# One set of key transposes a step later, the last head's products among the output projection's, and a norm broadcast three products later, in a two-layer hybrid attention trunk

## The chip, the cores and the metric

The kernel runs on one core of a Trainium2 chip. The metric is the device time of one execution in microseconds (us). Within a core five engines run side by side, each taking its own instructions strictly in their written order: PE multiplies matrices into PSUM banks, ACT applies functions and copies, DVE does element-wise arithmetic, POOL does the same for small side work, and SP starts the DMA transfers.

## What is computed

Two layers on 256 tokens of width 1024, in float32:

```python
h = h + 0.5 * swiglu(rms_norm(h, ffn1_norm[l]), ffn1_w_gate[l], ffn1_w_up[l], ffn1_w_down[l])
h = h + hybrid_mixer(rms_norm(h, mix_norm[l]), w_in[l], ..., w_out[l], cos, sin)
h = h + 0.5 * swiglu(rms_norm(h, ffn2_norm[l]), ffn2_w_gate[l], ffn2_w_up[l], ffn2_w_down[l])
```

A feed-forward block (FFN) has hidden width 2816. The mixer projects once with `w_in` and then has three head groups: A, four query heads that attend to the 64 keys per query which an indexer with eight small heads picks; B, four heads with plain causal attention at this length; C, eight heads with a forget bias and an output gate. Their 16 outputs are joined and multiplied by `w_out`.

## The kernel before

**Precision.** Each float32 matrix is split into a rounded part and a remainder (`wh`, `wl` for weights, `xhl` or `h`, `l` for activations), and three products stand for one. Weights come in by DMA as `raw`; ACT writes `wh` (L116), DVE subtracts to get `wl` (L120). `W.pump()` issues one such pair, up to seven units ahead of use; `W.take()` hands a unit to PE.

**Order.** It is written by hand: the order of the Python calls is the order on each engine. PSUM has eight banks, handed out in turn from two groups of four, "gu" and "acc"; a bank is written again only when its last readers are done.

**FFN.** For each of 22 tiles of the hidden width, `proj()` makes eight 512-wide products with `wh` and eight 256-wide ones with `wl` into one "gu" bank, once for the gate and once for the up matrix. The norm's scale is applied late: `norm.sums` (squares summed by PE), then a power on POOL (`y_n`, L304), then `norm.broadcast`, two small PE products that spread the scale over all partitions, copied by ACT into `rb` (L349). In every FFN but the first, `sums` is issued inside the first up group and `broadcast` inside the second gate group, each as a callback after one of the `wl` products. `gated` multiplies by `rb`.

**Mixer.** The projection runs in eight chunks of four units; after each unit a step counter goes up and `run_side` issues whatever is due at that step, in order of due time and then of registration, then one `W.pump()`. So the attention of group B and the indexer of A lie between the projection's products. The due steps that matter here: the last indexer sums and `cumsum` (which writes a bank that DVE reads at L763 and L764) at 16; `topk` rounds, two maxima and two replacements on DVE (L739, L741), at 17, 19, 21 and so on; `bq_turn` and `bk_turn` at `B_TURN` = 18; the first scores of B at 20. `bq_turn` multiplies the stacked queries by an identity (`identr`). `bk_turn` is `keys_T` with two "acc" banks: per bank four PE transposes (L626), an ACT cast (L628) and a DVE subtraction (L629), giving `bkT` high and low.

**End of the mixer.** A loop over the 12 heads of A and C interleaves their scores, `flip` (transposes of the probabilities, L920, copied as `pT`, L922), `values` (probabilities times values, then a reciprocal and scaling on DVE) and `outT` (two heads' outputs transposed, L953, and split by ACT L960 and DVE L961) with the output projection's first five inputs. `tail` does the last three inputs for the four pairs of output tiles (`mp` 0 to 3): products, then `residual` on DVE (L352), `nxt.high` on ACT (L317), `nxt.low` on DVE (L320), and the squares for the next norm. The last input needs the last `outT`, so for the first two pairs the products of the other two inputs are issued ahead of it:

```python
        if late:
            part(0, ks[:-1])
            late()
            part(1, ks[:-1])
        for mp in range(4):
            ms = (2 * mp, 2 * mp + 1)
            part(mp, ks[-1:] if late and mp < 2 else ks)
```

The next FFN's first `proj` follows directly; it takes inputs 0 to 5 first and 6 and 7 afterwards.

Of the kernel before, what the change touches and what calls it, by code (L numbers as in the profile page):

```python
# [36 lines left out]
OUT_TAIL = 3  # L37
WARM = 7
B_TURN, B_STEP, A_ROOT, A_TURN = 18, 20, 22, 26
# [12 lines left out]
OUT_ORDER = [2, 3, 0, 1, 4, 5, 6, 7]  # L52
# [88 lines left out]
def kernel(ctx: ExitStack, tc: tile.TileContext, x, ffn1_norm, ffn1_w_gate, ffn1_w_up, ffn1_w_down,  # L141
# [17 lines left out]
    def bank(tag):  # L159
        return psum.tile([P, 512], F32, name="ps_" + tag, tag=tag)  # L160

    def tmp(n):
        return tp.tile([P, 512], F32, name="tmp", tag="tmp")[:, :n]
# [128 lines left out]
    def mm(o, l, r, start, stop):  # L292
        T.matmul(o, l, r, start=start, stop=stop, skip_group_check=True)  # L293

    def mm3(o, lhs, rhs, start, stop):
        mm(o, lhs[0], rhs[0], start, False)
        mm(o, lhs[0], rhs[1], False, False)
        mm(o, lhs[1], rhs[0], False, stop)
# [52 lines left out]
    def residual(acc, m, n, factor):  # L351
        V.scalar_tensor_tensor(hres[:, m:m + n], acc[m // 2].rearrange("p (a b) -> p a b", a=2)[:, m % 2:m % 2 + n],  # L352
                               factor, hres[:, m:m + n], op0=ALU.mult, op1=ALU.add)


    def ffn(norm, nxt, aside=None, g0=None):
# [50 lines left out]
        def proj(between=None, after=0, tag="gu", groups=(range(KT),)):  # L407


            w = W.take()  # L410
            ps = bank(tag).rearrange("p (a b) -> p a b", a=2)
            for ks in groups:
                for k in ks:
                    mm(ps, w[0][:, k], norm.x[:, k], k == 0, False)
                for k in ks:
                    mm(ps[:, 0], w[1][:, k], norm.h[:, k], False, k == KT - 1)
                    if between and k == after:
                        between()
            return ps
# [35 lines left out]
        if first:  # L455
            u0 = proj()
            g1 = proj(norm.sums, 6)
            W.pump()
            W.low()
            for mp in range(1, 4):  # L460
                V.tensor_copy(hres[:, 2 * mp:2 * mp + 2], xT[mp])
            u1 = proj(norm.broadcast, 6)
            W.pump(2)
            early[2] = proj(tag="acc")
        else:
            g0 = proj(groups=(range(6), range(6, KT)))
            W.pump()
            u0 = proj(norm.sums, 5)
            W.pump(2)
            g1 = proj(norm.broadcast, 4)  # L470
            W.pump()
            u1 = proj()
        early[1] = g1
# [5 lines left out]
        acc = [bank("acc") for _ in range(4)]  # L479
        for f in range(1, NF):  # L480
# [6 lines left out]
            if f == 8 and aside:  # L487
                aside()
        ks = list(range(NF - DOWN_LAG, NF))
        return tail(acc, hid, ks, 0.25, nxt) if nxt else finish(ks)  # L490

    def tail(acc, rhs, ks, factor, make_norm, late=None):

        nxt = make_norm()
        ws = dict(zip(ks, [W.take() for _ in ks]))

        def part(mp, some):
            for k in some:
                for m in (2 * mp, 2 * mp + 1):
                    mm3(acc[mp][:, (m % 2) * S:(m % 2 + 1) * S], [v[:, 0, m * P:(m + 1) * P] for v in ws[k]],  # L500
                        rhs[k], False, k == ks[-1])

        if late:
            part(0, ks[:-1])
            late()
            part(1, ks[:-1])
        for mp in range(4):
            ms = (2 * mp, 2 * mp + 1)
            part(mp, ks[-1:] if late and mp < 2 else ks)
            for m in ms:  # L510
                if mp == 3:
                    residual(acc, m, 1, factor)
                elif m == ms[0]:
                    residual(acc, m, 2, factor)
                nxt.high(m)
            if late and mp == 0:
                continue
            for m in ((0, 1) if late and mp == 1 else ()) + ms:
                nxt.low(m)
            for p in (([0] if late and mp == 1 else []) + ([mp - 1] if mp > 1 or (mp == 1 and not late) else [])  # L520
                      + ([3] if mp == 3 else [])):
                nxt.squares(p)
        W.pump()
        return nxt
# [23 lines left out]
    def mixer(l, norm, nxt):  # L548
# [3 lines left out]
        def at_step(n, fn):  # L552
            side.append((n, next(count), fn))
# [7 lines left out]
        def heads(ap, n):  # L561
            return ap.rearrange("p (h d) -> p h d", h=n)

        def rope(x, ta, tb, E=G):

            n = x.shape[1]
            bc = lambda a: a[:, None, :].to_broadcast([P, n, a.shape[1]])
            b = tp.tile([P, S], F32, name="swapped", tag="swapped", bufs=2)
            b = heads(b[:, :n * HD], n)
            G.tensor_tensor(b[:, :, 0:32], x[:, :, 32:64], bc(tb[:, 0:32]), op=ALU.mult)  # L570
            G.tensor_tensor(b[:, :, 32:64], x[:, :, 0:32], bc(tb[:, 32:64]), op=ALU.mult)
            E.tensor_tensor(x, x, bc(ta), op=ALU.mult)
            E.tensor_tensor(x, x, b, op=ALU.add)
# [6 lines left out]
        def squares(ps, t, n):  # L580
            sq = tmp(64 * n)
            A.activation(sq, ps, AF.Square, scale=norm.r[:, t:t + 1])
            return heads(sq, n)

        def square_sums(ss, sq):
            V.tensor_reduce(ss, sq, axis=AX.X, op=ALU.add)

        def head_rs(ss, n, tag):
            return rsqrt(ss, ss, 1.0 / HD, n, tag)
# [6 lines left out]
        def evac(dst, ps, t, scale=None):  # L596
            A.activation(dst, ps, AF.Copy, scale=norm.r[:, t:t + 1])
# [206 lines left out]
        def post_b(ps):  # L804
            ss = sm.tile([P, 2, 4], F32, name="ssbk", tag="ss")
            rot = [hp.tile([P, S], F32, name="bkr", tag="hl") for _ in range(2)]
            sq = []
            for t in range(2):
                evac(rot[t], ps[t][:, :256], t)
                evac(va[t][:, 1:5, 0:64], heads(ps[t][:, 256:512], 4), t)  # L810
                sq.append(squares(ps[t][:, :256], t, 4))
                rope(heads(rot[t], 4), tab[:, 3, 0, t], tab[:, 3, 1, t])

            def bk_norm():
                for t in range(2):
                    square_sums(ss[:, t], sq[t])
                rs = head_rs(ss.rearrange("p t h -> p (t h)"), 8, "bk")
                for t in range(2):
                    twice = tmp(512).rearrange("p (h s d) -> p h s d", h=4, s=2)
                    G.tensor_tensor(twice, heads(rot[t], 4)[:, :, None, :].to_broadcast([P, 4, 2, HD]),  # L820
                                    rs[:, 4 * t:4 * t + 4, None, None].to_broadcast([P, 4, 2, HD]), op=ALU.mult)
                    bk.append(twice.rearrange("p h s d -> p h (s d)"))

            def bk_turn():
                st["bkT"] = at.tile([P, 2, 4, S], F32R, name="bkT", tag="kT")
                keys_T(st["bkT"], bk)

            bk = []
            at_step(13, bk_norm)
            at_step(B_TURN, bk_turn)  # L830

            def qk_b(kind, h):
                return st["bqT"][:, h], [st["bkT"][:, c, h] for c in range(2)]

            run_heads([("B", h) for h in range(4)], qk_b, "acc", lambda i, fn: at_step(B_STEP + i, fn), 2)
# [137 lines left out]
        oT = {}  # L973
        posts = dict(iq=post_iq, ib=post_ib, a=post_a, b=post_b, ck=post_ck, cq=post_cq, cv=post_cv, cg=post_cg)
        for name, cols in CHUNKS:
            n = sum(c[1] for c in cols)
# [20 lines left out]
        acc = [bank("acc") for _ in range(4)]  # L997
# [32 lines left out]
        scores, exps, flip, values, outT = run_heads(hs, qk_ac, "gu")  # L1030
        n = len(hs)
        next(halves)
        for i in range(n + 1):
            if i < n:
                scores(i)
            if i > 0:
                flip(i - 1)
            if i < n:
                exps(i)
            if i in (3, 5, 7, 9):  # L1040
                c_T((i - 3) // 2)
            if i not in (3, 5, 9, n):
                next(halves)
            if i > 0:
                values(i - 1)
                if i > 2 and i % 2:
                    outT((i - 3) // 2)
        for _ in halves:
            raise AssertionError
        return tail(acc, oT, OUT_ORDER[8 - OUT_TAIL:], 1.0, nxt, lambda: outT(n // 2 - 1))  # L1050


    def before_mixer(l):
# [12 lines left out]
    norm = Norm(0, 0)  # L1066
# [35 lines left out]
    for mp in range(4):  # L1102
        ks = range(2 * mp, 2 * mp + 2)
# [30 lines left out]
    for l in range(DEPTH):  # L1134
        norm = ffn(norm, lambda: Norm(1, l), lambda: before_mixer(l), g0 if l == 0 else None)
        norm = mixer(l, norm, lambda: Norm(2, l))
        norm = ffn(norm, (lambda: Norm(0, l + 1)) if l + 1 < DEPTH else None)
# [35 lines left out]
```

## Time and profile before

| what | us |
|---|---|
| median of 3 runs (lowest, highest) | 1061.42 (1061.30, 1061.51) |
| the profiled execution | 1061.49 |
| its span from first to last instruction | 1059.7 |
| PE busy | 1049.7 |
| DVE busy | 829.2 |
| ACT busy | 594.1 |

The profile records one execution. A timeline row has the start in us from the span's beginning, the time, the engine, the line, the operation, output and inputs, and the count of instructions merged into the row; in brackets stands how long the engine stood idle before it and what ended that. A row of the waits has the waiter, who released it, the sum, the count and the longest. A windows row has, for each engine, busy time and instruction count, then the granted TensorE clock, DMA share and GB/s. Mean granted clock over the run is 0.998.

### The profile page before, as it was taken

To read this page: it belongs to the slowest core of one execution; us is meant where nothing else is said; L and a number is where in the kernel's file an instruction comes from. 1 tells how busy PE (TensorE), PEld (TensorE's weight loads), DVE (VectorE), ACT (ScalarE), POOL (GpSimd) and SP (SyncE) were. 2 spreads that over 40 slices of the span, in tenths; PEclk is the share of its full clock that TensorE was granted. 3 is DMA by queue.
4 is the path that set the end of the run, shared out by engine and by line. 5 is a ranking of instruction groups with operands and counts; after the bars stand their busy time and mean duration, and the time that the engine had idled before them with its cause. 6 is when DMAs were issued, how large, how long until landed. Compare 5 with 4: busy or idle time off the path is not lost.

```text
span 1059.7 us, 16913 instructions
## 1 busy us (share of the span) xinstructions
PE 1049.7 (99%) x6611; PEld 950.5 (90%) x6611; DVE 829.2 (78%) x1568; ACT 594.1 (56%) x1018; POOL 164.1 (15%) x184
## 2 busy tenths in 40 slices
PE   9999999999999999999999999999999999999998
PEld 8999999998899899999989999999978998888887
DVE  6998777779876887777789777778798779877774
ACT  6665554667654665555456555547766555655551
POOL 2004000267700100000010300003765000000000
PEclk9999999999999999999999999999999999999999
DMA  9576464465441365464546555454455214564531
GB/s 328 202 242 202 161 228 154 133 221 169 134 148 41 120 238 187 171 220 143 195 159 221 183 200 188 171 185 167 159 170 185 84 41 163 198 234 163 198 119 40
DMA packets 130913, 181.81 MB, mean 172 GB/s; under 512 B 7009, under 2 KB 104721, under 8 KB 130833
## 3 DMA queue, kind: packets, MB, share of 16 engines
q1 hardware_dynamic: 130512, 180.65, 50.4%
q8 instruction: 52, 0.85, 0.3%
q14 instruction: 29, 0.23, 0.1%
q10 hardware_dynamic: 320, 0.08, 0.0%
HBM read 179.67 MB, written 1.05 MB: 171 GB/s over the span
## 4 chain that ended last, share of the span: by engine, by line
PE 62%; DVE 2%; ACT 1%; issue 1%; POOL 0%; POOLq 0%; ACTq 0%; DVEq 0%
PE ps_gu L293 41%; PE ps_acc L293 20%; DVE score L721 0%; PE ps_gu L920 0%; PE ps_gu L1020 0%; DVE wl L120 0%; DVE xhl L320 0%; DVE hres L352 0%; ACT xhl L317 0%; PE ps_acc L383 0%; ACT tmp L329 0%; POOLq L1169 0%; POOL y_n L304 0%; PE ps_gu L953 0%; PE ps_acc L920 0%
## 5 line engine op out<-in xcount | busy, mean ns | idle before, releaser
L120 DVE TENSOR_TENSOR wl<-raw,wh 128x1024 fp32r<-128x1024 f32 (+2 forms) x343 | 416.0, 1219 | 21.8 <-ACT wh L116 21.8
L293 PE MATMUL ps_gu<-xhl,wh 128*128 128x512 f32 (+1 forms) x1408 | 351.9, 392 | 0.2 <-DVE tmp L425 0.2
L116 ACT CAST wh<-raw 128x1024 fp32r<-128x1024 f32 (+2 forms) x343 | 344.6, 1033 | 7.6 <-PE ps_gu L293 3.3
L293 PEld LDWEIGHTS ps_gu<-xhl,wh 128*128 128x128 f32 x1408 | 253.8, 189 | 46.0 <-DVE tmp L425 0.4
L293 PEld LDWEIGHTS ps_gu<-xhl,wl 128*128 128x128 f32 x1400 | 192.1, 191 | 13.7
L293 PE MATMUL ps_gu<-xhl,wl 128*128 128x256 f32 x1400 | 198.0, 283 | 0.0
L293 PE MATMUL ps_gu<-wh,xhl 128*128 128x512 f32 (+2 forms) x512 | 159.5, 382 | 0.0
L425 DVE TENSOR_TENSOR tmp<-ps_gu,tmp 128x256 f32<-128x256 f32 x175 | 74.0, 423 | 106.6 <-ACT tmp L424 106.5
L293 PE MATMUL ps_acc<-hl,wh 128*128 128x256 f32 x528 | 150.0, 284 | 0.0
L293 PE MATMUL ps_acc<-hh,wl 128*128 128x256 f32 x528 | 149.7, 283 | 0.0
L293 PE MATMUL ps_acc<-hh,wh 128*128 128x256 f32 x528 | 149.6, 283 | 0.0
L424 ACT COPY tmp<-ps_gu 128x256 f32<-128x256 f32 x175 | 64.6, 369 | 132.8 <-PE ps_gu L293 126.9
L293 PEld LDWEIGHTS ps_gu<-wh,xhl 128*128 128x128 f32 x512 | 95.7, 190 | 14.7
L293 PEld LDWEIGHTS ps_acc<-hl,wh 128*128 128x128 f32 x528 | 101.5, 192 | 0.3
L293 PEld LDWEIGHTS ps_acc<-hh,wh 128*128 128x128 f32 x528 | 101.5, 192 | 0.0
L293 PEld LDWEIGHTS ps_acc<-hh,wl 128*128 128x128 f32 x528 | 101.5, 192 | 0.0
L293 PE MATMUL ps_gu<-wl,xhl 128*128 128x512 f32 (+2 forms) x256 | 96.5, 377 | 0.0
L331 POOL TENSOR_TENSOR ssacc<-ssacc,tmp 128x512 f32<-128x512 f32 x10 | 13.0, 1296 | 510.8 <-ACT tmp L329 332.2
L432 ACT ACTIVATE tmp<-tmp 128x256 f32<-128x256 f32 x88 | 36.8, 418 | 85.2 <-DVE tmp L430 85.2
L441 ACT CAST hh<-tmp 128x256 fp32r<-128x256 f32 x80 | 32.6, 408 | 86.6 <-DVE tmp L437 86.6
L293 PEld LDWEIGHTS ps_gu<-wl,xhl 128*128 128x128 f32 x256 | 48.7, 190 | 6.7
L430 DVE TENSOR_TENSOR tmp<-tmp,rb 128x256 f32<-128x256 f32 x88 | 37.8, 429 | 3.0
(247 smaller groups left out, 1231.8 us busy)
## 6 DMA issues: line engine op xcount, KB each, us to landing
raw<-in_ffn_w_down_dram SPq DMA_DIRECT2D x44, 1024.0 KB, 7.2
raw<-in_ffn_w_gate_dram SPq DMA_DIRECT2D x43, 1024.0 KB, 7.4
raw<-in_ffn_w_up_dram SPq DMA_DIRECT2D x43, 1024.0 KB, 5.0
raw<-in_w_in_dram SPq DMA_DIRECT2D x24, 1024.0 KB, 5.0
raw<-in_w_out_dram SPq DMA_DIRECT2D x8, 1024.0 KB, 4.8
raw<-in_w_in_dram SPq DMA_DIRECT2D x4, 768.0 KB, 4.8
raw<-in_w_in_dram SPq DMA_DIRECT2D x4, 656.0 KB, 4.4
xin<-in_x_dram SPq DMA_DIRECT2D x4, 256.0 KB, 5.0
```

The costliest lines, as they stand in the source:

```text
L116: self.nc.scalar.copy(hv, src)
L120: (engine or self.nc.vector).tensor_tensor(lv, self.srcs[self.n_low], hv.bitcast(F32), op=ALU.subtract)
L293: T.matmul(o, l, r, start=start, stop=stop, skip_group_check=True)
L331: G.tensor_tensor(self.acc, self.acc, sq, op=ALU.add)
L424: A.copy(o, ps[:, 1])
L425: V.tensor_tensor(o, ps[:, 0], o, op=ALU.add)
L430: V.tensor_tensor(t_, t_, norm.rb, op=ALU.mult)
L432: A.activation(th, t_, AF.Tanh, scale=0.5)
L441: (V.tensor_copy if late else A.copy)(hh, t_)
```

## The change

Three edits, each acting in several places. `bk_turn` moves from step 18 to step 19, where it is registered behind that step's `topk`; this happens in both mixers. In the loop over heads the last `values` is no longer issued right behind the last `flip`; `tail` now issues the early products of three pairs, with the last `values` behind those of pair 0, the last `outT` behind those of pair 1 and nothing behind those of pair 2; this too happens twice. And `norm.broadcast` is issued behind the last `wl` product of the second gate group, no longer behind the fifth, in three FFNs. On DVE only the order around the key turn changes; on ACT one `wh` cast goes ahead of the two key casts; the order on POOL and SP stays.

```diff
@@ ffn
             u0 = proj(norm.sums, 5)
             W.pump(2)
-            g1 = proj(norm.broadcast, 4)
+            g1 = proj(norm.broadcast, 7)
@@ tail
-        if late:
-            part(0, ks[:-1])
-            late()
-            part(1, ks[:-1])
+        for mp, fn in enumerate(late or ()):
+            part(mp, ks[:-1])
+            fn()
         for mp in range(4):
             ms = (2 * mp, 2 * mp + 1)
-            part(mp, ks[-1:] if late and mp < 2 else ks)
+            part(mp, ks[-1:] if late and mp < len(late) else ks)
@@ mixer, post_b
             at_step(13, bk_norm)
-            at_step(B_TURN, bk_turn)
+            at_step(B_TURN + 1, bk_turn)
@@ mixer, loop over heads
-            if i > 0:
+            if 0 < i < n:
                 values(i - 1)
...
-        return tail(acc, oT, OUT_ORDER[8 - OUT_TAIL:], 1.0, nxt, lambda: outT(n // 2 - 1))
+        return tail(acc, oT, OUT_ORDER[8 - OUT_TAIL:], 1.0, nxt,
+                    (lambda: values(n - 1), lambda: outT(n // 2 - 1), lambda: None))
```

## The prediction

> **What bounds the kernel now.** First the page's engine times, then the waits of PE.
>
> ```profile
> span 1059.7 us, 16913 instructions
> PE 1049.7 (99%) x6611; PEld 950.5 (90%) x6611; DVE 829.2 (78%) x1568; ACT 594.1 (56%) x1018; POOL 164.1 (15%) x184
> ```
>
> ```profile
> PE ps_acc L626 <- DVE cka L764: 3.2, 2, 1.6
> PE ps_gu L293 <- ACT pT L922: 1.2, 2, 0.6
> ...
> PE ps_acc L293 <- POOL y_n L304: 0.6, 3, 0.3
> ```
>
> PE is busy for 99% of the span, so the kernel is PE's list of products plus the few moments when PE stands still. The three edits aim at the three rows above: the key transposes wait for a bank (3.2 us in two mixers), the last `values` waits for its copied probabilities (1.2 us in two), the broadcast waits for POOL (0.6 us in three FFNs). Together that is 5.0 us. What each edit is worth is decided by what ends last just behind it, and there DVE, 78% busy on average, has long stretches without a gap. So I read the timeline at each of the places, PE and DVE against each other. PE, first mixer:
>
> ```profile
> 247.51 1.00 PE L293 MATMUL ps_acc<-identr,stacked 128*128 128x128 f32 x8
> 248.35 0.62 PE L626 MATMUL ps_acc<-cst,tmp 128*128 128x128 f32 x4
> 250.60 0.63 PE L626 MATMUL ps_acc<-cst,tmp 128*128 128x128 f32 x4 [1.63 <-DVE cka L764]
> 250.99 0.48 PE L293 MATMUL ps_gu<-wh,xhl 128*128 128x512 f32 x1
> ...
> 256.52 0.62 PE L293 MATMUL ps_acc<-bkT,bqT 128*128 128x128 f32 x4
> ```
>
> DVE at the same place:
>
> ```profile
> 250.30 0.16 DVE L764 TENSOR_SCALAR cka<-ps_acc 128x8 f32<-128x8 f32 x1
> ...
> 252.93 1.21 DVE L120 TENSOR_TENSOR wl<-raw,wh 128x1024 fp32r<-128x1024 f32 x1
> 254.06 1.27 DVE L629 TENSOR_TENSOR bkT<-ps_acc,bkT 128x512 fp32r<-128x512 f32 x2
> 255.26 1.52 DVE L120 TENSOR_TENSOR wl<-raw,wh 128x1024 fp32r<-128x1024 f32 x1
> 256.69 0.61 DVE L739 MAX8 m<-score 128x8 f32<-128x128 f32 x2
> ...
> 257.87 1.21 DVE L120 TENSOR_TENSOR wl<-raw,wh 128x1024 fp32r<-128x1024 f32 x1
> ```
>
> The reader is to see that DVE lags. None of these rows has an idle time in brackets; each starts as the one before it ends. The `bkT` subtractions belong to step 18, which PE reached at 247.5, yet DVE comes to them at 254.06. PE's first scores of B, which need them, start at 256.52, when the first half has been done since about 254.7 and the second since 255.3. That margin of one to two us is all there is.
>
> **Key turn, first mixer.** The move carries eight transposes, two ACT casts and two DVE subtractions past one unit of products on PE (12 products), one `wh` cast on ACT, and on DVE past one `wl` and one whole `topk` round. It issues no DMA, and the order on SP and POOL stays.
>
> The old wait goes: the bank is free at 250.30 + 0.16, and with the 0.14 us until PE's start at 250.60 that is 250.6; the transposes now come one unit (256.52 - 250.99 = 5.53 for two, so 2.77) behind 248.35, at 251.1. PE then stands at the first scores at 256.52 - 1.63 = 254.9.
>
> What is late next is `bkT`. DVE does not depend on PE here, so it still ends its previous round at 252.93, and then has: `wl` (to 254.06, 1.13 us), the next `wl` (1.13 by that row, or 255.26 to 256.69 = 1.43; I take 1.28, as both occur), the `topk` round (256.69 to 257.87 = 1.18), and the first `bkT` subtraction (half of 1.27, 0.64). With 0.14 until PE starts: 252.93 + 1.13 + 1.28 + 1.18 + 0.64 + 0.14 = 257.30. So a wait of 2.4 us takes the place of one of 1.63. Against the old start, 256.52, this is 0.78 later; the first product of the group needs only the high half and runs ahead of the wait, about 0.1, so the cost is **+0.70 us**. Ends: +0.5 with the shorter `wl`, +1.4 if the group has to wait for both subtractions. It can't be a gain, since no instruction of DVE's queue is removed ahead of `bkT`. Behind it, DVE comes to the scores' scan after one more `wl`, at 259.0 as before, so nothing is lost a second time.
>
> **Key turn, second mixer.**
>
> ```profile
> 770.81 1.01 PE L293 MATMUL ps_acc<-identr,stacked 128*128 128x128 f32 x8
> 771.65 0.62 PE L626 MATMUL ps_acc<-cst,tmp 128*128 128x128 f32 x4
> 773.89 0.63 PE L626 MATMUL ps_acc<-cst,tmp 128*128 128x128 f32 x4 [1.61 <-DVE cka L764]
> 774.27 0.67 PE L293 MATMUL ps_gu<-wh,xhl 128*128 128x512 f32 x1
> ...
> 781.44 0.62 PE L293 MATMUL ps_acc<-bkT,bqT 128*128 128x128 f32 x4
> ```
>
> ```profile
> 776.21 1.21 DVE L120 TENSOR_TENSOR wl<-raw,wh 128x1024 fp32r<-128x1024 f32 x1
> ```
>
> ```profile
> 250.00:254.00 4.00, 3.40 (x17) 2.94 (x18) 4.00 (x13) 2.49 (x3) 3.84 (x6) 1.00 0.24 50
> 774.20:774.40 0.20, 0.20 (x4) 0.20 (x3) 0.20 (x1) 0.00 (x0) 0.20 (x1) 0.96 0.00 0
> 777.60:777.80 0.20, 0.20 (x2) 0.10 (x2) 0.20 (x1) 0.00 (x0) 0.20 (x2) 0.50 1.08 420
> 777.80:778.00 0.20, 0.20 (x3) 0.15 (x1) 0.20 (x2) 0.00 (x0) 0.20 (x1) 1.00 1.02 399
> ```
>
> The same on DVE: 776.21 + 1.13 + 1.28 + 1.18 + 0.64 + 0.14 = 780.58. But here PE came to the first scores only at 781.44, for behind the old wait the granted clock was 0.50 from 774.38 (0.96 over 0.2 us means 8% of it slow) to 777.80, 3.42 us that cost half, 1.71 us. Where the scores no longer stand behind that stretch, they start at 780.58, less 0.1 as above: **-0.94 us**, made up of +0.77 for the longer wait and -1.71 for the clock, if the new wait doesn't bring the clock down again.
>
> Does it? The first mixer had the same wait, 1.63 against 1.61, and its clock stayed at 1.00 in the windows row above. Both lie in a stretch without ordinary products, 247.51 to 250.99 and 770.81 to 774.27, as only identity products and transposes stand before and within them. If the clock is judged in fixed windows of 3.42 us, the slow one was decided by 770.96 to 774.38, with 0.11 us of ordinary products in it; 153 windows of 3.413 us earlier lies 248.73 to 252.14, with 1.15 us of them (from 250.99), and it passed. The new wait of 2.4 us has ordinary products on both sides, so any 3.42 us holds at least 1.0 of them. That is far nearer to the one that passed, so I take no slow stretch behind the new wait; the other end is 1.71 us for each mixer.
>
> [...]
>
> **Last head's values, end of both mixers.** PE and DVE, first mixer:
>
> ```profile
> 335.77 0.88 PE L293 MATMUL ps_gu<-va,pT 128*128 128x65 f32 x6 [0.62 <-ACT pT L922]
> 336.46 0.36 PE L293 MATMUL ps_acc<-oh,wh 128*128 128x256 f32 x1
> ...
> 337.97 0.38 PE L953 MATMUL ps_gu<-cst,o 128*128 128x128 f32 x2
> 338.11 0.36 PE L293 MATMUL ps_acc<-oh,wh 128*128 128x256 f32 x1
> ...
> 339.62 0.40 PE L293 MATMUL ps_acc<-ohl,wh 128*128 128x256 f32 x2
> ...
> 347.49 0.72 PE L293 MATMUL ps_gu<-xhl,wh 128*128 128x512 f32 x2
> ```
>
> ```profile
> 340.55 1.41 DVE L352 SCALAR_TENSOR_TENSOR hres<-ps_acc,hres 128x512 f32<-128x512 f32 x2 [1.33 <-PE ps_acc L293]
> ...
> 346.59 1.06 DVE L320 SCALAR_TENSOR_TENSOR xhl<-hres,gT,xhl 128x256 fp32r<-128x256 f32 x2 [0.25 <-ACT xhl L317]
> ```
>
> The wait of 0.62 goes: twelve products (338.11 to 339.62, 1.51 us) now stand between the flip and `values`, more than the copy needs. What is late next is the tail. The first `residual` waits for the last product of pair 0. Before, that group of six began at 339.62. Now PE does, from 335.77 - 0.62 = 335.15 on, block 0 (1.51), `values` (336.46 - 335.77 = 0.69), block 1 (1.51), `outT` (0.14) and block 2 (1.51): 340.51, so 0.89 later. DVE and ACT then do one chain, residuals, highs and lows turn about, whose order is unchanged and which is DVE's own from 340.55 to the last low at 346.59 + 1.06 = 347.65. All of it moves by 0.89, to 348.54. PE alone would be 0.62 earlier, but its product with input 7, before at 347.49 + 0.23 = 347.72, needs the last low. There were 0.07 us between them. So PE starts it near 348.6: **+0.87 us** where -0.62 was meant. Ends: +0.82 if all 0.07 was slack, +0.89 if none; if ACT and DVE could close the 0.25 us before the last lows, +0.6.
>
> The second mixer has it in the same places, 872.14 + 0.23 = 872.37 against 871.24 + 1.06 = 872.30:
>
> ```profile
> 871.24 1.06 DVE L320 SCALAR_TENSOR_TENSOR xhl<-hres,gT,xhl 128x256 fp32r<-128x256 f32 x2 [0.25 <-ACT xhl L317]
> ```
>
> ```profile
> 872.14 0.72 PE L293 MATMUL ps_gu<-xhl,wh 128*128 128x512 f32 x2
> ```
>
> Two times +0.87 is **+1.74 us**.
>
> **Broadcast.**
>
> ```profile
> 354.27 0.71 PE L293 MATMUL ps_acc<-cst,y_n 128*128 128x128 f32 x4 [0.18 <-POOL y_n L304]
> ...
> 357.95 2.00 PE L293 MATMUL ps_gu<-xhl,wh 128*128 128x512 f32 x8
> ```
>
> ```profile
> 356.64 0.42 DVE L425 TENSOR_TENSOR tmp<-ps_gu,tmp 128x256 f32<-128x256 f32 x1 [0.72 <-ACT tmp L424]
> ```
>
> Three more products of 0.12 (a twelfth of the 1.51 above) now stand ahead of the broadcast, 0.36. That is more than the 0.18 here and the longest of the three in the row of the waits, 0.3, so that row goes: **-0.6 us**. `rb` comes up to 0.36 later against PE. Behind ACT's copy wait a `wh` cast and the gate's copy, and DVE frees that bank at 356.64 + 0.42 = 357.06; two whole groups stand before PE wants it again, at 357.95, so 0.9 hides the delay. Without that cover the edit would gain nothing; that is the upper end, 0.
>
> **The sum.** +0.70 - 0.94 + 1.74 - 0.6 = +0.9 us. The profiled execution took 1061.49, 0.07 over the median of the runs: 1062.4, against the median 1062.3, which I give. All low ends together, 0.5 - 1.1 + 1.2 - 0.6, leave 1061.5; the high ends, 0.85 - 0.8 + 1.8 + 0, make 1063.3.
>
> **Rivals.** *All three waits simply go*, and the clock stays up: 3.2 + 1.2 + 0.6 + 1.7 = 6.7 us less, 1054.7. Against it stand the gapless DVE rows before `bkT` and the 0.07 us before input 7; 4%. A half of it, with the tail as meant and the key turn as I have it, gives 0.9 - 1.74 - 1.24 = -2.1, 1059.3; 4%. *The new wait brings the clock down*: one mechanism, at the first scores of B, 1.71 us each time. It decides at the amount of ordinary products a window needs: had the limit been above 1.0 us and the wait fallen wholly within one window, one drop gives 1064.0, two 1065.8. The one that passed had 1.15, so the limit lies between 0.11 and 1.15 and this is open; where the windows will fall is not known either. I give one drop 23% and two 9%. *The edit doesn't do what it says*, the transposes still waiting for the bank: it is free at 250.6 and they come at 251.1, half a microsecond late enough; 2%, near 1063.5.
>
> **How the numbers follow.** The forecast has 58%. 0.2% of the time, 2.1 us, is what I count as no change, about what a measurement of this kernel can tell from none. The forecast and its ends lie within it. Slower by more takes a clock drop, 32%, and a small part of the rest; faster takes the first rivals, 7%. The range goes from 1061.2 to 1064.3, which holds the forecast and one drop.
>
> **What would show it.** In the profile after: no wait at L626 for `cka`; a wait of about 2.4 us at the products of `bkT` and `bqT`, released by DVE L629, in both mixers; clock 1.00 behind it; no wait for `pT` at the end of the mixers, but PE standing some 0.8 us or more in the next FFN's first group, for `xhl` L320; no wait for `y_n`. Wrong would be no wait at the scores, or none for `xhl`, or a clock of 0.5 behind the scores.

## The result: 1.9 us slower, and the profile after

| | median us | lowest, highest | executions |
|---|---|---|---|
| before | 1060.81 | 1059.55, 1061.81 | 22 |
| changed | 1062.74 | 1061.04, 1064.36 | 22 |

The ratio is 1.0023 with a 95% interval of 1.0016 to 1.0029. The times of both kernels lie in steps of 1.3 to 1.6 us, and each execution's mean granted clock tells which step: 1.000 or 0.999 with no stretch at half clock, 0.998 with one, 0.997 with two. (The profiles at 0.998, before and changed, have one such stretch of 3.41 us; that 0.997 means two is worked out from it: twice 1.71 us lost in 1061 is 0.3%.) Of the changed kernel's 22 executions one had none (1061.04), eleven had one (mean 1062.54) and ten had two (mean 1064.09). The 22 of before lie, by their times, in two groups of eleven, around 1060.1 and around 1061.5. The median of before falls in the gap between the two, so the difference of the means, 2.4 us, says more than the 1.9 of the medians. At an equal number of half-clock stretches the change costs about 1.0 us, and it has more such stretches, 31 in 22 executions against about 11, which makes about 1.4 us in the mean.

The waits of PE in the changed kernel:

```profile
PE ps_acc L293 <- DVE bkT L629: 4.2, 2, 2.1
PE ps_gu L293 <- DVE xhl L320: 1.3, 4, 0.4
PE ps_gu L293 <- POOL minus_half L182: 1.0, 1, 1.0
PE ps_gu L293 <- DVE tmp L425: 0.2, 1, 0.2
```

The three rows at which the edits aimed are gone. Two new ones stand in their place, both released by DVE: the first scores of B wait for the keys' low half, and the next FFN's first gate group waits for the normalised input. The last two rows were there before.

PE at the key turn of the first mixer, transposes and scores:

```profile
247.66 1.00 PE L293 MATMUL ps_acc<-identr,stacked 128*128 128x128 f32 x8
...
251.34 1.04 PE L626 MATMUL ps_acc<-cst,tmp 128*128 128x128 f32 x8
...
254.95 0.22 PE L293 MATMUL ps_acc<-bkT,bqT 128*128 128x128 f32 x1
257.29 0.61 PE L293 MATMUL ps_acc<-bkT,bqT 128*128 128x128 f32 x3 [2.12 <-DVE bkT L629]
```

DVE there:

```profile
253.11 2.35 DVE L120 TENSOR_TENSOR wl<-raw,wh 128x1024 fp32r<-128x1024 f32 x2
255.38 0.61 DVE L739 MAX8 m<-score 128x8 f32<-128x128 f32 x2
...
256.56 1.27 DVE L629 TENSOR_TENSOR bkT<-ps_acc,bkT 128x512 fp32r<-128x512 f32 x2
257.75 1.21 DVE L120 TENSOR_TENSOR wl<-raw,wh 128x1024 fp32r<-128x1024 f32 x1
```

PE turns the keys without a stop, runs one product of the scores and stands until DVE has worked off two `wl`, a `topk` round and half of `bkT`. All four rows of DVE follow on one another without a gap.

A little further on PE gets some of it back. From B's last scores to the flip behind its first `values` it took 1.33 us before and takes 1.08 now. First before, then in the changed kernel:

```profile
266.43 0.62 PE L293 MATMUL ps_acc<-bkT,bqT 128*128 128x128 f32 x4
...
267.76 0.50 PE L920 MATMUL ps_acc<-cst,p 128*128 128x128 f32 x3
```

```profile
267.20 0.62 PE L293 MATMUL ps_acc<-bkT,bqT 128*128 128x128 f32 x4
...
268.28 0.50 PE L920 MATMUL ps_acc<-cst,p 128*128 128x128 f32 x3
```

The `values` in between need the copy `pT`, which ACT starts at 266.53 before and at 266.54 now. I read the 0.25 us, which the list of the waits does not show, as a stop for this copy: before, PE was there early, and now it comes late enough.

The second mixer has the same wait, and behind it the granted clock (third column from the right) goes to half:

```profile
780.79 0.61 PE L293 MATMUL ps_acc<-bkT,bqT 128*128 128x128 f32 x3 [2.12 <-DVE bkT L629]
```

```profile
778.00:780.00 2.00, 0.67 (x4) 0.37 (x2) 2.00 (x7) 0.00 (x0) 1.92 (x3) 1.00 1.03 392
781.80:782.00 0.20, 0.20 (x2) 0.13 (x1) 0.20 (x1) 0.00 (x0) 0.20 (x1) 0.50 0.99 410
784.00:785.00 1.00, 1.00 (x3) 0.73 (x3) 0.28 (x1) 1.00 (x2) 0.46 (x1) 0.50 0.00 0
786.00:788.00 2.00, 2.00 (x11) 1.69 (x10) 1.77 (x10) 2.00 (x5) 0.00 (x0) 1.00 0.92 373
```

The slow stretch, 781.79 to 785.21, follows the new wait. The profiled execution had it behind the second mixer's wait only; about half of the others had two by their mean clock.

Why one wait of 2.12 us did and the other did not is, as I read it, a matter of place. In these profiles the clock changes at times that lie whole multiples of 3.413 us apart. In the changed kernel they are 781.79, 785.21 and, behind the last instruction, 1061.69, so 1 and 81 times; in before 774.38, 777.80 and 1061.10, 1 and 83 times; with the longer wait below 257.86, 264.68, 786.92 and 793.75, 2, 153 and 2 times. From one profile to another they do not: 774.38 and 781.79 are 7.41 apart. I call such a grid's stretch of 3.413 us a window. Carried back from 781.79, the grid has one from 778.38 to 781.79, which holds the second wait (778.67 to 780.79) whole; in the first mixer a boundary at 256.14 cuts the wait (255.17 to 257.29) into 0.97 and 1.15 us, and the clock stayed at 1.00. That the part of a wait within one window decides is my supposition: the profiles show where the waits and the changes lie, not what sets the clock.

The end of the first mixer, PE and then DVE:

```profile
335.19 0.49 PE L920 MATMUL ps_gu<-cst,p 128*128 128x128 f32 x3
335.43 0.36 PE L293 MATMUL ps_acc<-oh,wh 128*128 128x256 f32 x1
...
346.36 0.89 PE L293 MATMUL ps_gu<-xhl,wh 128*128 128x512 f32 x2 [0.22 <-DVE xhl L320]
...
348.41 0.90 PE L293 MATMUL ps_gu<-xhl,wh 128*128 128x512 f32 x2 [0.45 <-DVE xhl L320]
```

```profile
341.65 1.41 DVE L352 SCALAR_TENSOR_TENSOR hres<-ps_acc,hres 128x512 f32<-128x512 f32 x2 [1.33 <-PE ps_acc L293]
...
347.62 1.14 DVE L320 SCALAR_TENSOR_TENSOR xhl<-hres,gT,xhl 128x256 fp32r<-128x256 f32 x2 [0.24 <-ACT xhl L317]
```

PE goes on 0.24 us after the flip's start, but DVE's first residual is at 341.65 and its last low ends at 348.76; PE waits for the lows twice.

### The profile page after: what moved, and what is told of

The parts are those of the page before. It is cut to its first block, busy times and chain, and to the rows that moved or that the text cites. A ratio compares the mean times of both kernels' runs of the same rounds, so it can differ in the third digit from the quotient of the medians.

```text
span 1060.8 us, 16910 instructions
## 1 busy us (share of the span) xinstructions
PE 1050.5 (99%) x6611; PEld 950.2 (90%) x6611; DVE 828.2 (78%) x1568; ACT 594.6 (56%) x1018; POOL 166.1 (16%) x184
## 3 DMA queue, kind: packets, MB, share of 16 engines
HBM read 179.67 MB, written 1.05 MB: 170 GB/s over the span
## 4 chain that ended last, share of the span: by engine, by line
PE 93%; DVE 4%; ACT 2%; issue 1%; POOL 0%; ACTq 0%; POOLq 0%
PE ps_gu L293 61%; PE ps_acc L293 29%; DVE wl L120 1%; DVE score L721 1%; PE ps_gu L920 1%; DVE xhl L320 1%; PE ps_gu L1020 0%; DVE hres L352 0%; ACT wh L116 0%; PE ps_gu L953 0%; PE ps_acc L920 0%; ACT L703 0%; ACT L701 0%; DVE score L741 0%; PE ps_acc L1076 0%
## 5 line engine op out<-in xcount | busy, mean ns | idle before, releaser
L437 DVE TENSOR_TENSOR tmp<-tmp 128x256 f32<-128x256 f32 x88 | 37.6, 427 | 3.0
```

The lines of the kernel that those rows point to most:

```text
L437: V.tensor_tensor(t_, summed(u), t_, op=ALU.mult)
```

## The experiments

In each, "before" is the kernel before, run on the same chip beside it. Two sets of four kernels were run; before had 28 executions in the first (18 without a half-clock stretch, mean 1060.25; 10 with one, 1061.54) and 21 in the second (10, mean 1060.23; 11, mean 1061.57).

**The key turn alone.**

```diff
-            at_step(B_TURN, bk_turn)
+            at_step(B_TURN + 1, bk_turn)
```

> The key turn alone (step 19 instead of 18). Theory (a queue in the way): PE's wait for the bank goes and a wait of 2.1 us for DVE's bkT at the first scores of B takes its place in both mixers, since DVE has one more wl and one topk round ahead of it. Measured by PE's starts that is +0.4 us in each mixer. The longer wait also brings the clock down more often than the old one, 1.5 us each time. So against a run of before with the same number of clock drops +0.8, and over the runs +1 to +2.5 us. Rival (all of the loss sits in the tail): the key turn alone is level or gains up to 3 us.

1062.80 us (six executions, 1060.63 to 1065.93), ratio 1.0024 (1.0010 to 1.0038). One execution without a half-clock stretch took 1060.63, three with one 1062.68 in the mean, two with two 1065.31. The wait for `bkT` is there in both mixers, and here it is the first behind which the clock falls:

```profile
257.12 0.61 PE L293 MATMUL ps_acc<-bkT,bqT 128*128 128x128 f32 x3 [2.11 <-DVE bkT L629]
...
782.42 0.62 PE L293 MATMUL ps_acc<-bkT,bqT 128*128 128x128 f32 x3 [2.12 <-DVE bkT L629]
```

```profile
258.00:259.00 1.00, 1.00 (x5) 0.78 (x4) 1.00 (x4) 0.00 (x0) 1.00 (x2) 0.83 1.01 418
```

The row's 0.83 puts the fall at 258.66. The window that ends there holds 1.87 us of the wait and 1.54 of products; in the second mixer a boundary at 780.90 cuts the wait, the larger part is 1.52, and the clock stayed up. If the waiting within one window decides, these two put the limit for a fall among ordinary products between 1.52 and 1.87 us, an estimate from two waits of one profile. By PE's starts in the profile, everything behind the first mixer's key turn comes 1.97 us later, of which about 1.6 is the half clock and 0.4 the wait. The rival, that the key turn is harmless, is out.

**The tail alone.**

```diff
-        if late:
-            part(0, ks[:-1])
-            late()
-            part(1, ks[:-1])
+        for mp, fn in enumerate(late or ()):
+            part(mp, ks[:-1])
+            fn()
...
-            if i > 0:
+            if 0 < i < n:
...
-        return tail(acc, oT, OUT_ORDER[8 - OUT_TAIL:], 1.0, nxt, lambda: outT(n // 2 - 1))
+        return tail(acc, oT, OUT_ORDER[8 - OUT_TAIL:], 1.0, nxt,
+                    (lambda: values(n - 1), lambda: outT(n // 2 - 1), lambda: None))
```

> The last values and the last flip among the output products alone. Theory (DVE's chain starts later): no wait for pT, but the first residual comes 0.6 us later in both mixers and PE waits for xhl (some 0.2 and 0.45 us) in the next FFN's first group: +1.2 us, with clock drops as in before. Rival (the wait removed is simply gained): -1.2 to -1.7 us and no wait for xhl.

1062.25 us (eleven, 1060.88 to 1065.36), ratio 1.0014 (1.0005 to 1.0023). Without a half-clock stretch 1061.05 (five) against 1060.25, with one 1062.54 (five) against 1061.54: 0.8 to 1.0 us slower at equal clocks (one execution had two stretches, 1065.36). By PE's starts each mixer's end costs 0.58. The waits show how it is paid:

```profile
PE ps_acc L625 <- DVE cka L763: 3.3, 2, 1.6
PE ps_gu L293 <- DVE xhl L320: 1.3, 4, 0.4
```

The wait for `pT` is gone, the one for `xhl` has come, and the bank's wait is that of before (L763 and L764 stand next to each other on DVE). So this edit is a loss by itself.

**The broadcast alone.**

```diff
-            g1 = proj(norm.broadcast, 4)
+            g1 = proj(norm.broadcast, 7)
```

> The broadcast behind the whole gate group alone. Theory (a wait costs its shown idle time plus about 0.25 us, because the idle time is counted from the modelled end of the last product and not from when the next could start): -0.35 to -0.45 us in each of three FFNs, -1.2 us in all. Rival (it is worth what the row of the waits shows): -0.6 us. Rival (the later rb is passed on): 0.

1059.38 us (eleven, 1058.92 to 1061.00), ratio 0.9990 (0.9981 to 0.9999). Without a half-clock stretch 1059.2 against 1060.25, with one 1060.6 against 1061.54, so 0.9 to 1.1 us gained; by PE's starts 0.33 in each of the three FFNs. That is more than the 0.2 each of the row of the waits and near the theory's 0.35 to 0.45. It is the one edit of the three that pays.

**Queries later and not keys.**

```diff
-            at_step(B_TURN, bq_turn)
+            at_step(B_TURN + 1, bq_turn)
```

> Another order than the change's: the keys stay at step 18 and are turned there alone, the queries go to step 19, so that the two key banks are ones that ACT has freed, and the bank that DVE frees late falls to the queries, a unit later. The order on DVE is that of before. Theory: the wait at L626 goes, bkT is ready on DVE where it was before, near 254.7, just where PE now comes, so at most 0.2 us of wait is left; PE gains 1.8 us in each mixer and the clock never drops: -3.6 us against an execution of before without a drop (1060.1), so near 1056.5. Rival (the wait moves on to the first scores in full): the gain is under 1 us. Rival (the clock drop does not come from this wait): some runs keep a drop of 1.5 us.

1062.05 us (eleven, 1059.95 to 1064.90), ratio 1.0016 (1.0007 to 1.0025): a miss. PE came to the first scores 1.55 us earlier than before, each counted from its own start, and did not wait there, as forecast. It waited a few products on, and behind that nothing of the 1.55 was left. PE, and then ACT in the first mixer:

```profile
266.79 0.88 PE L293 MATMUL ps_acc<-va,pT 128*128 128x65 f32 x6 [1.54 <-ACT pT L922]
```

```profile
265.54 0.40 ACT L913 ACTIVATE p<-tmp,nm 128x128 f32<-128x128 f32 x1 [0.61 <-DVE nm L906]
265.86 0.51 ACT L914 ACTIVATE p<-tmp,nm 128x256 f32<-128x256 f32 x1
266.27 0.46 ACT L922 COPY pT<-ps_acc 128x384 f32<-128x384 f32 x1
```

The copy of the flipped probabilities stands on ACT behind exponentials that wait for DVE's scan. DVE has next to no time to spare in this stretch (busy 17.7 of the 18 us from 250 to 268), so here the whole wait that was taken from PE came back at the next thing that hangs on DVE. The half clock came behind this wait too, at 268.11 in the profile; by their mean clocks two executions had no such stretch, five had one and four had two.

**The topk rounds out of DVE's way**, in the changed kernel.

```diff
-                at_step(17 + 2 * r, topk)
+                at_step((23, 25, 26, 27, 28, 29, 30, 31)[r], topk)
```

> The changed kernel, with the eight topk rounds at steps 23 and 25 to 31 and not at 17, 19 up to 31, so that DVE has neither the round of step 17 nor that of step 19 ahead of bkT. Theory (DVE's queue makes the new wait, and the wait brings the clock down): the wait at the first scores falls from 2.1 us to under 0.3, no wait elsewhere in the stretch takes its place, and no execution shows a clock drop: 4 us below an execution of the changed kernel without a drop (1061.0), near 1057. Rival (DVE is behind anyway and the wait moves on, to pT of B or to the first scores of A): less than 2 us. Rival (the clock drop has another cause): drops stay in most executions.

1057.94 us (eleven, 1057.59 to 1059.87), ratio to before 0.9974 (0.9966 to 0.9983). DVE in the first mixer:

```profile
250.66 3.85 DVE L120 TENSOR_TENSOR wl<-raw,wh 128x1024 fp32r<-128x1024 f32 x3
254.44 1.28 DVE L629 TENSOR_TENSOR bkT<-ps_acc,bkT 128x512 fp32r<-128x512 f32 x2
```

`bkT` starts 2.1 us earlier than in the changed kernel, the wait for it is gone from the list, and no execution has a half-clock stretch (all 1.000). The gain over the changed kernel's one execution without such a stretch is 3.1 us, where 4 was expected (2.8 by the mean: two of the eleven, 1059.59 and 1059.87, were slower at the same clock, and why is open). Of the 1.9 us that PE was ahead of the kernel before at the end of B in the first mixer, 0.8 was lost again by the first flips of A, 0.34 of it at a new wait of A's key transposes for a bank that DVE frees. So the theory holds, and the rival, that a part moves on, holds for that part.

**A longer wait.** The key turn alone, with three additions on DVE ahead of `bkT` whose result nobody uses:

```diff
+                dump = at.tile([P, 2, 512], F32, name="dump", tag="sg")
+                for _ in range(3):
+                    V.tensor_tensor(dump[:, 0, :3 * P], causal, causal, op=ALU.add)
                 st["bkT"] = at.tile([P, 2, 4, S], F32R, name="bkT", tag="kT")
```

> The key turn alone (as in the change), with three additions of 384 columns on DVE ahead of bkT, whose result nobody uses. The wait at the first scores grows by some 1.3 us, to about 3.4, in both mixers. Theory (fixed windows of 3.4 us, in which the share of time without products decides): every execution now drops the clock in both mixers, 1.5 us each: near 1066.3, all runs alike. Rival (a drop is chance and not set by the wait): some executions with no drop or one, as with 2.1 us, and 1063.3 for those without.

1070.84 us (four, 1070.41 to 1071.28), ratio 1.0096 (1.0081 to 1.0112). The additions took 2.43 us and not 1.3, so the wait became 4.5 us:

```profile
PE ps_acc L293 <- DVE bkT L629: 9.0, 2, 4.5
```

```profile
257.00:258.00 1.00, 0.00 (x0) 0.00 (x0) 0.97 (x2) 0.00 (x0) 0.92 (x2) 0.93 0.78 213
260.00:262.00 2.00, 2.00 (x7) 1.71 (x8) 2.00 (x5) 0.11 (x1) 0.16 (x1) 0.50 0.04 12
262.00:264.00 2.00, 2.00 (x6) 1.61 (x5) 1.40 (x3) 2.00 (x4) 0.00 (x0) 0.50 0.00 0
264.00:265.00 1.00, 1.00 (x4) 0.76 (x4) 0.00 (x0) 1.00 (x3) 0.00 (x0) 0.66 0.76 90
266.00:268.00 2.00, 2.00 (x10) 1.66 (x9) 2.00 (x11) 1.69 (x4) 0.00 (x0) 1.00 0.88 363
```

The slow stretch lasts from 257.86 to 264.68, 6.82 us and not 3.41, and so does the second mixer's (786.92 to 793.75). All four executions are alike, with mean clock 0.994. Counted by the waits, the share that brought the clock down goes up with their length: 21 of 98 waits of 1.6 us in the 49 executions of before, 31 of 44 waits of 2.1 us in the changed kernel, 8 of 8 of 4.5 us. The counts take each stretch that a mean clock shows to go with one of these waits, as it does in the profiles. The time was 4.5 us higher than expected, about half of it from the longer waits and the rest from slow stretches twice as long, which the theory did not have.

**The early products dealt out otherwise**, keys and broadcast as before.

```diff
-            part(0, ks[:-1])
-            late()
+            part(0, ks[:1])
+            late[0]()
+            part(0, ks[1:-1])
+            late[1]()
             part(1, ks[:-1])
...
+                    (lambda: values(n - 1), lambda: outT(n // 2 - 1)))
```

> The tail with the early products dealt out otherwise: six products of pair 0 stand between the last flip and the last values, the other six of pair 0 between values and outT, the twelve of pair 1 between outT and the last input, and none of pair 2 comes early. Keys and broadcast as before. Theory (what counts is when the first residual starts, for DVE's chain from there to the last xhl is what the next FFN waits for): the wait for pT shrinks to nothing, the first residual starts some 0.7 us earlier than before, and PE keeps all of it: -1.4 us for two mixers at equal clock drops. Rival (any product put between flip and values delays the tail as in the change): +0.5 us or more and a wait for xhl.

1060.10 us (eleven, 1058.84 to 1060.79) beside 1061.17 of before, ratio 0.9991 (0.9982 to 1.0000). At equal clocks: 1058.93 against 1060.23 and 1060.35 against 1061.57, so 1.2 to 1.3 us gained where 1.4 was expected (the second pair gives 1.05 without one execution of before at 1063.16). DVE:

```profile
339.91 1.41 DVE L352 SCALAR_TENSOR_TENSOR hres<-ps_acc,hres 128x512 f32<-128x512 f32 x2 [1.33 <-PE ps_acc L293]
...
345.96 1.06 DVE L320 SCALAR_TENSOR_TENSOR xhl<-hres,gT,xhl 128x256 fp32r<-128x256 f32 x2 [0.25 <-ACT xhl L317]
```

The first residual starts 0.64 us earlier than before, the last low 0.63 earlier, and PE, which waits for neither `pT` nor `xhl`, is 0.6 us earlier in the next FFN. The end of the mixer is one chain from the last flip to the last low, and products help there only as far as they fill its pauses.

**Four edits together.** Queries later (a miss alone), the `topk` rounds later, the tail dealt out in sixes, the broadcast at 7.

> Keys turned at step 18 ahead of the queries, which go to step 19; the topk rounds at 23 and 25 to 31; the tail dealt out in sixes; the broadcast behind the whole gate group. Theory: no wait at L626, at the first scores, for pT or for y_n, and no clock drop; against an execution of before without a drop (1060.2): -1.8 in each mixer for the key turn, -0.7 in each for the tail, -1.1 for the broadcasts: -6.1, near 1054.1. Rival (DVE, behind in that stretch, gives a wait further on): above 1057.

1055.31 us (five, 1055.09 to 1055.81), ratio 0.9950 (0.9938 to 0.9963): 4.9 us under before without a half-clock stretch, where 6.1 was expected, and it has none itself (0.999 and 1.000). It beats both kernels. The waits for the key bank, `bkT`, `pT`, `xhl` and `y_n` are all out of its list, and 0.7 us is left in two waits of A's key transposes for a bank. As in the kernel with the later `topk`, PE's lead shrinks on the way to A's first scores, in the first mixer from 2.0 to 1.2 us. What the later queries add to the later `topk` was not measured apart.

## Why the prediction was right, and where it was not

The direction and the range held: 1062.74 measured, 1062.3 forecast, 1061.2 to 1064.3 given. The mechanisms of the key turn and the tail were the forecast ones. But the sum came out near by errors of opposite sign, which is luck.

- **Key turn, +0.70.** The wait at the first scores, its releaser and its start in DVE's queue were right (257.29 against 257.30). At the scores the cost was 0.60: the next unit of products starts at 257.74 and not at 256.99, with PE 0.15 later from the start. What the term left out is the second stop at B's first `values`, where 0.25 came back, so that the edit costs 0.35 in this mixer. (The sum of the high ends took 0.85 for this term where the term itself names 1.4; with 1.4 it makes 1063.9, still in the range.)
- **Clock, -1.71: the step that failed.** The prediction took no half-clock stretch behind the new wait, as every window would hold at least 1.0 us of ordinary products. That the products in a window decide was my supposition, and no run shows it. In the changed kernel's profile the slow stretch starts at 781.79, and the 3.41 us ahead of it, less the wait of 2.12, hold 1.3 us of them, more than the 1.15 of the window that passed before; with the key turn alone a window with 1.54 us dropped too. The one that passed had 0.63 us of identity products and transposes besides. So if windows decide, these count for something, and my limit between 0.11 and 1.15 rested on their counting nothing. Seven in ten waits of 2.1 us dropped the clock (31 of 44). On the same supposition an estimate from the 1.52 and 1.87 us of the key turn alone and a grid of 3.413 us that may fall anywhere gives 53 to 73% for a wait of 2.12 us. The rival "the new wait brings the clock down", given 32%, is what happened.
- **The time before.** The profile had one half-clock stretch, and so, by their times, had the three runs that I had; half of the 22 executions had none. I took for the kernel's time what was one of its two steps.
- **Last values, +0.87 in each mixer.** Measured +0.58: the old wait was worth more than its row, since PE resumed 0.24 us behind the flip's start (335.19 to 335.43) and not 0.49 as I had from the row's idle time. The residual moved by 0.57 and not 0.89, net of what came before it. The chain to the last low then passed all of it on, as forecast.
- **Broadcast, -0.6.** Measured alone -0.9 to -1.1, again a wait worth more than its idle time. The cover that I named held.

At an equal number of half-clock stretches my terms without the clock, 0.70 + 0.77 + 1.74 - 0.6, make +2.6; the runs show about 1.0. By PE's starts in the two profiles, with one half-clock stretch in each, it is made up of +0.4 and +0.6 at the key turns, +0.6 at each mixer's end and -0.4, -0.3 and -0.4 at the broadcasts. So each of my terms lay too high: the key turn's by the second stop (read in the first mixer), the other two by the size of the removed wait. With -1.71 for a stretch that did not stay away, that came to the +0.9 of the forecast; the measured +1.9 is +1.0 of waits and the rest of more half-clock stretches. That the three edits together are the sum of each (+0.4 to +1.1, +0.8 to +1.0 and -0.9 to -1.1 at equal clocks) fits the runs to within their spread, with one execution behind some of the numbers.

What stays open: whether the waiting within a window is what brings the clock down, and what identity products, transposes and narrow products count for in it. A wait of 1.54 us among transposes and narrow products, in the kernel with the queries later, dropped it in 13 of 22 cases by the mean clocks, while 1.6 us behind identity products did in 21 of 98.

## What to carry to other kernels

Before moving work to fill a wait, follow the queue of the engine that releases it: where that engine ran without a gap here, the wait only changed its place (1.6 us at the key bank became 2.1 at the first scores, or 1.5 at the first `values`), and moving other work out of the way in its queue (the `topk` rounds, 3.1 us at equal clocks) is what paid. What a removed wait is worth is read from the time between the starts of the instructions around it less the work between them, and from where PE waits next, rather than from the idle time in its row: at the tail 0.87 for a row of 0.62, at the broadcast 0.33 for about 0.2. At the key bank, where the row says 1.63, PE came to the first scores 1.55 to 1.73 us earlier in three kernels without that wait (queries later, `topk` later, four edits together). At the end of a stage, look for the chain that the next stage waits for, and put in no more work than fills its pauses: dealt out in sixes the early products gained 1.2 to 1.3 us, in twelves they lost 0.8 to 1.0.

## What the hardware showed that I had not expected

Waits of 2.1 us, with ordinary products on both sides, brought the granted clock from 1.00 to 0.50 for 3.41 us in 31 of 44 cases by the mean clocks, 1.3 to 1.6 us each; waits of 1.6 us did in 21 of 98. In the profiles the clock changed at times that lie whole multiples of 3.413 us apart. Cut along this grid, the two waits behind which it fell had 2.12 and 1.87 us within one window, the two behind which it stayed up 1.15 and 1.52 (the changed kernel, the key turn alone); that this part decides is my reading of four waits. Two executions of one program differ by 1.5 or 3 us (the changed kernel: 1061.04, and around 1062.54 and 1064.09), and three executions can all lie on one step (before: 1061.30 to 1061.51). And three additions of 384 columns on DVE took 2.43 us, 0.8 each, where I had expected 1.3 for the three.
